# A hybrid SSD and sparse-attention block on one core: the first gate/up pair's products reordered, two operand sums split beside the output projection, the last pair written plainly, the ring moved in four parts, weight memory divided differently

## The chip, the cores and the metric

The kernel runs on one core of a Trainium2 chip. The metric is device time in microseconds (us) of one execution. The engines of the core are named as the profile names them: PE (TensorE matmul), PEld (its weight load), DVE (VectorE), ACT (ScalarE), POOL (GpSimd) and SP (SyncE, which here only issues DMAs). ACT and POOL issue DMAs too.

## The reference

One layer with a batch of 1, 512 tokens, 2048 features, in float32. The first part of the block (projection, SSD mixer, three-branch attention) is the same in both kernels. What matters here is what follows it:

```python
def reference(x, attn_norm_w, w_in, ..., w_out, ffn_norm_w, w_gate, w_up, w_down, final_norm_w):
    h = x
    u = rmsnorm(h, attn_norm_w[l])
    ...
    y_ssd = ssd_mixer(z, xbc, dt_raw, ...)          # 512 x 1024
    y_att = nsa_mixer(q, kc, vc, ks, vs, kw, vw, ...) # 512 x 1024
    mixed = jnp.concatenate([y_ssd, y_att], axis=-1)
    h = h + mixed @ w_out[l]                          # 2048 x 2048
    v = rmsnorm(h, ffn_norm_w[l])
    h = h + (jax.nn.silu(v @ w_gate[l]) * (v @ w_up[l])) @ w_down[l]   # 2048 x 5632, 5632 x 2048
    return rmsnorm(h, final_norm_w)
```

## The kernel before

**Every product is three.** A float32 operand is split into a high part (`a_hi`, ACT, rounds to fp32r) and a low part (`lo`, DVE, the difference to it), and a block of a product is accumulated from high x high, high x low and low x high: lines L1119, L1120 and L1121, one row of 128 x 128 weights at a time.

**The feed-forward part uses seven products for eight.** The matrices are cut into 2 x 2 quarters, and gate, up and down are each computed by seven products `M1` to `M7` of sums of quarters. On the side of the tokens the seven operands are `V0`, `VV` (two) and four sums `T` (index 0 to 3), which POOL forms during the output projection and which are split into high and low parts before the first pair. On the side of the weights the sums are `S1`, `S3`, 11+S1 and 12+11+S1. `S1` and `S3` of gate and up come by a plain DMA and a second, accumulating DMA that POOL issues (L1067). The two others are DVE adds (`plus`, L126).

**Stages.** The input projection, SSD and attention run until about 800 us of the profile, the output projection until about 900. Then come 22 pairs, each of a gate side and an up side of 7 steps (`NP` = 22 tiles of the hidden width). A step is 24 matmuls of 256 columns. The result of a pair, its seven operands for the down projection split in high and low, goes to DRAM as one tile of 1792 KB (`g_d`, `g_forms`). The down projection follows in 36 visits: `VISITS` lists (output block j, number n of hidden tiles), and a visit has seven steps of 3n matmuls.

**The ring.** The down projection reads the tiles of `g_d` back into seven slots (`GRING`), which are the memory of `V0`, `VV` and `T`. `feed(i)` issues the read of tile n on ACT's DMA queue (L1413) two steps after the last step that reads what its slot held (`done`); the slots' order is `V_SLOT`. A read waits for that last step.

**Weights in flight.** Raw weights land in `F` (zone of `NZ` = 56 blocks of 128 x 128, of which the down projection may use the first `NZ2` = 44); the split weights are in `R` (56 blocks). `advance` issues loads on SP (L1065) in the order of `loads`, as soon as a place is free. `form` makes high parts up to three steps ahead, `prep` low parts up to two steps ahead. From the feed-forward part on, each engine's order is that in which the code is written (`manual_schedule`), so an instruction that waits holds up all that stands behind it on its engine.

**First and last pair.** `pair_at_once` runs the first four steps of the first and the last pair as M1, M1, M2, M2 of both sides, then the rest side by side. `start_ff(n)` splits the sums `T`: index 0 and 1 ahead of step 0, index 2 ahead of step 1, index 3 ahead of step 2.

Of the kernel before, what the change touches and what calls it, by code (L numbers as in the profile page):

```python
# [22 lines left out]
VISITS = [(0, 3), (1, 4), (2, 5), (3, 5), (4, 6), (5, 6), (6, 5), (7, 5), (0, 4), (1, 4), (7, 5), (5, 5), (6, 5), (2, 5),  # L23
          (3, 5), (4, 5), (0, 4), (1, 4), (7, 4), (0, 5), (6, 5), (5, 5), (3, 6), (2, 6), (4, 5), (1, 4), (7, 4), (6, 4),
          (0, 6), (1, 6), (7, 4), (2, 6), (6, 3), (5, 6), (4, 6), (3, 6)]
GRING = 7
# [25 lines left out]
NF, NZ, NZ2 = 124, 56, 44  # L52

# [54 lines left out]
def body(ctx, tc, xT, w_in, w_out, w_gate, w_up, w_down, w1k, w1v, cols, rows, kst, out):  # L108
# [46 lines left out]
    g_d = dram.tile([NP, 128, 7, 2, 256], F32, name="g_d")  # L155
# [830 lines left out]
    class Blk:  # L986
# [4 lines left out]
        def __init__(self, n, reads, src=None, plus=None, both=None, inplace=False):  # L991
            self.n, self.reads, self.src, self.plus, self.both, self.inplace = n, reads, src, plus, both, inplace
            self.at, self.down = None, False

        def ap(self):
            return fz.ap(self.at, self.n)

        def read(self):
            self.reads -= 1
            if not self.reads:  # L1000
                fz.free(self.at, self.n)
                self.at = None

    class Zone:


        def __init__(self, key, n):
            self.key, self.busy, self.age, self.now = key, [False] * n, [0] * n, 0
# [4 lines left out]
        def take(self, n, upto, starts=None):  # L1013

            b, g, got = self.busy, self.age, []
            for i in starts or range(upto - n + 1):
                edge = starts or i == 0 or b[i - 1] or i + n == upto or b[i + n] or g[i] != g[i - 1]
                if edge and not any(b[i:i + n]):
                    got.append((max(g[i:i + n]), i))
            if not got:  # L1020
                return None
            a = min(got)[1]
            self.busy[a:a + n] = [True] * n
            return a

        def free(self, i, n):
            self.now += 1
            self.busy[i:i + n] = [False] * n
            self.age[i:i + n] = [self.now] * n


    fz, hz = Zone("F", NZ), Zone("R", NZ)
# [10 lines left out]
    def advance():  # L1043
        while nxt["raw"] < len(loads):
# [3 lines left out]
            if b.inplace:  # L1048
                x, y = b.both
                b.at = x.at  # L1050
# [5 lines left out]
            b.at = place(b)  # L1056
            if b.at is None:
                return
            if b.both:
# [11 lines left out]

    def form(upto):

        while nxt["form"] <= min(upto, len(items) - 1):
            i = nxt["form"]
            b, plus = items[i]
            advance()
            assert b.at is not None, (i, fz.busy)
            if plus is not None:
                add(dve, b.ap(), b.ap(), plus.ap())  # L1080
                plus.read()
            hl[i] = [hl_place(b)]
            assert hl[i][0] is not None, (i, hz.busy)
            a_hi(hz.ap(hl[i][0], b.n), b.ap())
# [652 lines left out]
```

## Time and profile before

| | |
|---|---|
| median of 3 runs | 2320.18 us (2319.45 to 2322.86) |
| the profiled execution | 2321.24 us, its span 2319.3 us |
| busy in the span | PE 2215.3 us, PEld 2057.3, DVE 1803.0, ACT 1098.1, POOL 430.9 |
| DMA | 419.18 MB, 181 GB/s over the span |
| mean granted clock of TensorE | 0.974 |

The profile is of one execution, 2321.24 us long, which is 1.06 us above the median of the runs. About 2 us of it lie outside of the span. Busy shares are means over stages. In the feed-forward part PE's idle time lies in a few stretches, and there the wait that ended last is what counts.

### The profile page before, as it was taken

The page shows a single profiled execution, that of the slowest core. Times are in us where ns is not written, and L with a number is a line of the kernel's source. Part 1 is how long each engine was busy: PE and PEld are TensorE (multiplying, and loading weights), DVE is VectorE, ACT ScalarE, POOL GpSimd, SP SyncE. Part 2 cuts the span into 40 slices and gives each one's busy share as a digit, 9 for nine tenths or more (in the row PEclk, how much of TensorE's full clock was granted, in tenths as well). Part 3 has the DMA queues.
Part 4 walks back from the last instruction along what each step waited for, and adds up shares of the span by engine and source line. Part 5 has one row for each costly group of instructions (what it writes and reads, how often), then busy time and mean ns, then how long its engine had stood idle before and what let it go on. Part 6 is the DMA issues. An engine that isn't in the chain of part 4 may idle for free. (4 is left out here: it accounts for less than half of the span.)

```text
span 2319.3 us, 39808 instructions
## 1 busy us (share of the span) xinstructions
PE 2215.3 (96%) x15376; PEld 2057.3 (89%) x15376; DVE 1803.0 (78%) x2918; ACT 1098.1 (47%) x1767; POOL 430.9 (19%) x439
## 2 busy tenths in 40 slices
PE   7999999999989899999999999999998898999997
PEld 5888888888868678999999999999998898999986
DVE  7699766688797667788888878888785786878776
ACT  4564446566676444444444444444443343333443
POOL 2011334323222233000000010000000121211122
PEclk8999999999999899999999999999999999999998
DMA  4222342222224365878788787878786758676766
GB/s 175 89 69 76 126 137 99 68 89 71 71 83 149 127 220 147 219 216 252 216 250 223 229 235 218 240 210 250 216 251 220 304 168 282 195 258 193 258 162 167
DMA packets 135469, 419.18 MB, mean 181 GB/s; under 512 B 16448, under 2 KB 22096, under 8 KB 129648
## 3 DMA queue, kind: packets, MB, share of 16 engines
q1 hardware_dynamic: 99840, 251.91, 31.3%
q0 software_dynamic: 25776, 77.70, 17.4%
q10 hardware_dynamic: 9664, 87.04, 10.0%
q8 instruction: 120, 1.97, 0.3%
q14 instruction: 69, 0.57, 0.1%
HBM read 354.45 MB, written 58.20 MB: 178 GB/s over the span
## 5 line engine op out<-in xcount | busy, mean ns | idle before, releaser
L117 ACT ACTIVATE R<-F 128x1024 fp32r<-128x1024 f32 (+4 forms) x576 | 517.0, 912 | 668.9 <-DVE F L126 357.7
L120 DVE TENSOR_TENSOR R<-F,R 128x1024 fp32r<-128x1024 f32 (+4 forms) x576 | 610.6, 1067 | 37.8 <-ACT R L117 28.2
L224 PE MATMUL ps_g<-u_hi,whi 128*128 128x512 f32 x592 | 237.5, 401 | 0.0
L226 PE MATMUL ps_g<-u_hi,wlo 128*128 128x512 f32 x592 | 236.1, 399 | 0.0
L225 PE MATMUL ps_g<-u_lo,whi 128*128 128x512 f32 x592 | 235.7, 398 | 0.0
L1121 PE MATMUL ps_s<-T,R 128*128 128x256 f32 x698 | 203.0, 291 | 23.0 <-DVE R L120 23.0
L126 DVE TENSOR_TENSOR F<-F 128x1024 f32<-128x1024 f32 (+4 forms) x168 | 169.9, 1012 | 64.1 <-POOL F L126 39.6
L120 DVE TENSOR_TENSOR wlo<-wraw,whi 128x512 fp32r<-128x512 f32 x196 | 150.6, 771 | 71.2 <-ACT whi L117 70.2
L1121 PE MATMUL ps_g<-T,R 128*128 128x256 f32 x704 | 200.0, 284 | 2.1 <-DVE R L120 2.1
L1119 PE MATMUL ps_s<-T,R 128*128 128x256 f32 x698 | 201.2, 288 | 0.0
L1120 PE MATMUL ps_s<-T,R 128*128 128x256 f32 x698 | 201.1, 288 | 0.0
L1119 PE MATMUL ps_g<-T,R 128*128 128x256 f32 x704 | 199.3, 283 | 1.3 <-ACT R L117 1.1
L1120 PE MATMUL ps_g<-T,R 128*128 128x256 f32 x704 | 199.3, 283 | 0.0
L1121 PE MATMUL ps_t<-T,R 128*128 128x256 f32 x678 | 192.6, 284 | 0.4 <-DVE R L120 0.4
L1120 PE MATMUL ps_t<-T,R 128*128 128x256 f32 x678 | 192.0, 283 | 0.0
L1119 PE MATMUL ps_t<-T,R 128*128 128x256 f32 x678 | 192.0, 283 | 0.0
L117 ACT ACTIVATE whi<-wraw 128x512 fp32r<-128x512 f32 x196 | 122.4, 626 | 141.3 <-PE ps_g L225 92.1
L1121 PEld LDWEIGHTS ps_s<-T,R 128*128 128x128 f32 x698 | 136.7, 196 | 25.3 <-DVE R L120 25.1
L1119 PEld LDWEIGHTS ps_s<-T,R 128*128 128x128 f32 x698 | 136.7, 196 | 0.0
L1120 PEld LDWEIGHTS ps_s<-T,R 128*128 128x128 f32 x698 | 136.6, 196 | 0.0
L1121 PEld LDWEIGHTS ps_g<-T,R 128*128 128x128 f32 x704 | 133.8, 190 | 3.0 <-DVE R L120 2.9
L1119 PEld LDWEIGHTS ps_g<-T,R 128*128 128x128 f32 x704 | 133.6, 190 | 1.7 <-ACT R L117 1.3
(406 smaller groups left out, 6335.9 us busy)
## 6 DMA issues: line engine op xcount, KB each, us to landing
F<-in_w_gate SPq DMA_DIRECT2D x110, 512.0 KB, 5.1
F<-in_w_up SPq DMA_DIRECT2D x110, 512.0 KB, 7.1
wraw<-in_w_in SPq DMA_DIRECT2D x164, 256.0 KB, 3.0
g_d<-F ACTq DMA_DIRECT2D x22, 1792.0 KB, 6.7
F<-in_w_gate POOLq DMA_DIRECT2D x44, 512.0 KB, 6.1
F<-in_w_up POOLq DMA_DIRECT2D x44, 512.0 KB, 5.6
F<-in_w_down SPq DMA_DIRECT2D x68, 320.0 KB, 5.1
T<-g_d ACTq DMA_DIRECT2D x12, 1792.0 KB, 11.8
```

Of the source, the lines that this page charges most:

```text
L117: act.activation(dst, src, AF.Copy, scale=scale)
L120: eng.tensor_tensor(dst, src, f(hi), ALU.subtract)
L126: eng.tensor_tensor(o, a, b, ALU.add)
L224: pe.matmul(p, hi_t[i][:, j, :], ah, start=(k == 0), stop=False)
L225: pe.matmul(p, hi_t[i][:, j, :], al, start=False, stop=False)
L226: pe.matmul(p, lo_t[i][:, j, :], ah, start=False, stop=(k == u.nk - 1))
L1119: pe.matmul(q, h[:, k, :], ah, start=(k == 0), stop=False)
L1120: pe.matmul(q, h[:, k, :], al, start=False, stop=False)
L1121: pe.matmul(q, l[:, k, :], ah, start=False, stop=(k == s.blk.n - 1))
```

## The change

- The first pair's order is now M1, M1, M2, M2, M3, M3, then M6, M7, M5, M4 side by side. Its DVE sums are made for M3 (`sums`), its loads reordered (S1 ahead of 12), and the two steps of the norm (`step_r3`) stand at n = 1 and 4.
- `T` is split in halves (`t_piece`): the first halves of index 0 and 1 beside the output projection (`half_t`, in memory of their own, `ta`), the other six one by one ahead of steps 1 to 6.
- The last pair is written like the pairs in the middle; a slot counts as free after its up side.
- `g_d` is laid out in four slabs, and each DMA moves, per partition, four rows of 3584 bytes in place of one of 14336.
- `R` has 48 blocks in place of 56; 8 blocks `E` serve as further split weights until the down projection, and as further raw weights (`E2`) in it. Split weights in the down projection have eight places of 6 blocks, before it was seven.
- In the first six visits POOL forms S1 in new memory and S3 in place (before the other way round, S3 first). `VISITS` is another list.

```diff
-VISITS = [(0, 3), (1, 4), (2, 5), (3, 5), (4, 6), (5, 6), (6, 5), (7, 5), (0, 4), (1, 4), (7, 5), (5, 5), (6, 5), (2, 5),
...
+VISITS = [(0, 3), (1, 4), (2, 5), (3, 5), (4, 5), (5, 5), (6, 5), (7, 4), (0, 4), (7, 4), (4, 5), (1, 5), (6, 5), (2, 5),
...
+NR, NE = 48, 8
-    g_d = dram.tile([NP, 128, 7, 2, 256], F32, name="g_d")
+    g_d = dram.tile([NP, 4, 128, 896], F32, name="g_d")
...
+    fz, hz, ez = Zone("F", NZ), Zone("R", NR), Zone("E", NE)
     def place(b):
-        return fz.take(b.n, NZ2 if b.down else NZ)
+        n = b.n
+        if b.down:
+            return take(n, fz.find(n, NZ2), ez.find(n) if "E2" in P2 and n <= NE else None)
+        return take(n, fz.find(n))
     def hl_place(b):
-        return hz.take(b.n, NZ, range(0, 42, 6) if b.down else range(0, NZ, 8))
+        n = b.n
+        if b.down:
+            return take(n, hz.find(n, NR, range(0, NR - 5, 6))) or take(n, hz.find(n))
+        return take(n, hz.find(n, NR, range(0, NR, 8)), ez.find(n))
...
+            if c == 7:
+                sch.add(half_t())
+    def t_piece(i, h):
+        src = P2["T1"][h] if i == 0 else (P2["T2"] if i == 1 else P2["T34"][:, i - 2])[:, 4 * h:4 * h + 4]
+        o = P2["T"][i][:, 4 * h:4 * h + 4]
+        a_hi(o[:, :, 0, :], src)
+        lo(dve, o[:, :, 1, :], src, o[:, :, 0, :])
+        if i == 0:
+            fz.free(NZ - 16 + 8 * h, 8)
+    def half_t():
+        yield 12
+        t_piece(0, 0)
+        yield 16
+        t_piece(1, 0)
...
-        nc.scalar.dma_start(g_d[u], f(sg))
+        nc.scalar.dma_start(g_d[u].rearrange("q p n -> p q n"), f(sg).rearrange("p v s t -> p (v s t)").rearrange("p (q n) -> p q n", q=4))
...
+                t_piece(*[(0, 1), (1, 1), (2, 0), (2, 1), (3, 0), (3, 1)][n - 1])
...
+    loads += [qs[0, side][a] for a, side in (("11", 0), ("11", 1), ("S1", 0), ("12", 0), ("12", 1), ("S1", 1), ("S3", 0),
+                                             ("22", 0), ("S3", 1), ("22", 1))]
+    seq = [(0, M1), (1, M1), (0, M2), (1, M2), (0, M3), (1, M3)] + [(i, p) for i in range(2) for p in (M6, M7, M5, M4)]
...
+        if n in (1, 4):
+            ev = step_r3(ev)
...
-    for u in range(1, NP - 1):
+    for u in range(1, NP):
...
-    pair_at_once(NP - 1)
...
-            nc.scalar.dma_start(f(G[n]), g_d[n])
+            nc.scalar.dma_start(f(G[n]).rearrange("p v s t -> p (v s t)").rearrange("p (q n) -> p q n", q=4),
+                                g_d[n].rearrange("q p n -> p q n"))
...
-        add_loads(q, "11 12 21 22 S3 S1" if v < 6 else "11 12 21 22 S1 S3")
+        add_loads(q, "11 12 21 22 S1 S3")
```

Three places show how instructions move. The first is DVE at the start of the first pair, before (T_9071, T_9069, T_9070, T_9072 are index 0 to 3, rows `R<-F,R` the low parts of weights, `F<-F 128x1024` the adds of weight quarters):

```order
L126 TENSOR_TENSOR F<-ps_g,F 128x512
L1181 SCALAR_TENSOR_TENSOR F<-F,colc 128x512
L120 TENSOR_TENSOR T_9071<-F,T_9071 128x4x256 x2
L126 TENSOR_TENSOR acc_97<-ps_v,acc_97 128x512
L120 TENSOR_TENSOR VV<-F,VV 128x2x256
L120 TENSOR_TENSOR T_9069<-F,T_9069 128x8x256
L120 TENSOR_TENSOR R<-F,R 128x1024
L120 TENSOR_TENSOR T_9070<-F,T_9070 128x8x256
L126 TENSOR_TENSOR F<-F 128x1024
L120 TENSOR_TENSOR R<-F,R 128x1024
```

The same place of the changed kernel (T_8420 and T_8421 are index 0 and 1, T_9084 is index 2):

```order
L128 TENSOR_TENSOR F<-ps_g,F 128x512
L122 TENSOR_TENSOR R<-F,R 128x1024
L1204 SCALAR_TENSOR_TENSOR F<-F,colc 128x512
L128 TENSOR_TENSOR acc_97<-ps_v,acc_97 128x512
L122 TENSOR_TENSOR VV<-F,VV 128x2x256
L122 TENSOR_TENSOR T_8420<-F,T_8420 128x4x256
L128 TENSOR_TENSOR F<-F 128x1024 x2
L122 TENSOR_TENSOR R<-F,R 128x1024
L275 TENSOR_SCALAR rst<-ps_m 128x4
L125 TENSOR_TENSOR rst<-rst 128x4 x2
L122 TENSOR_TENSOR T_8421<-F,T_8421 128x4x256
L128 TENSOR_TENSOR F<-F 128x1024 x2
```

A low part of weights has moved up ahead of the sums, the sums come in halves, and the adds of two quarters stand where the adds of one stood.

The second is ACT in the last pair, before (`V`, `VV`, `T` with `<-g_d` are reads of the ring, `R<-F` high parts of weights, L1298 the silu after the gate side):

```order
L1329 DMA g_d<-F 128x3584
L1278 ACTIVATE F<-ps_t 128x256
L117 ACTIVATE R<-F 128x1024
L1413 DMA V_8415<-g_d 128x3584
L117 ACTIVATE R<-F 128x1024 x2
L1413 DMA VV<-g_d 128x3584
L117 ACTIVATE R<-F 128x1024 x4
L1298 ACTIVATE F<-F 128x1024
L117 ACTIVATE R<-F 128x1024 x2
L1413 DMA T_9069<-g_d 128x3584
```

The changed kernel at the same place:

```order
L1371 DMA g_d<-F 128x4x896
L119 ACTIVATE R<-F 128x1024 x5
L1340 ACTIVATE F<-F 128x1024
L119 ACTIVATE R<-F 128x1024
L1320 ACTIVATE F<-ps_g 128x256
L119 ACTIVATE R<-F 128x1024
L1444 DMA V_8415<-g_d 128x4x896
L119 ACTIVATE R<-F 128x1024
L1444 DMA VV<-g_d 128x4x896
L119 ACTIVATE R<-F 128x1024
L1444 DMA T_8421<-g_d 128x4x896
L1452 DMA F<-h_d 128x1024 x2
```

The first two reads of the ring have moved from ahead of the silu to behind it, into the up side, and the first three now follow each other at one step's distance.

The third is SP at the first loads of the down weights, before:

```order
L1065 DMA F<-in_w_up 128x1024 x3
L1065 DMA F<-in_w_down 128x384 x4
L1065 DMA F<-in_w_down 128x512 x4
L1065 DMA F<-in_w_down 128x640 x8
L1065 DMA F<-in_w_down 128x768 x8
L1065 DMA F<-in_w_down 128x640 x10
```

In the changed kernel (E_18322 is `E2`):

```order
L1081 DMA F<-in_w_up 128x1024 x5
L1081 DMA F<-in_w_down 128x384 x4
L1081 DMA F<-in_w_down 128x512 x4
L1081 DMA F<-in_w_down 128x640
L1081 DMA E_18322<-in_w_down 128x640
L1081 DMA F<-in_w_down 128x640 x6
L1081 DMA E_18322<-in_w_down 128x640
L1081 DMA F<-in_w_down 128x640 x12
```

About every sixth load goes to the new place, so one more block of a visit can be under way.

## Rows read from the trace of the kernel before

**Rows 1.** The page: busy tenths of PE in 40 slices of the span.

```profile
PE   7999999999989899999999999999998898999997
```

**Rows 2.** Busy time by stretch: length, engines (instructions), granted clock, DMA share, GB/s.

```profile
900.66:956.87 56.21, 47.14 (x349) 46.32 (x348) 40.81 (x42) 24.30 (x24) 10.47 (x10) 0.88 0.62 160
1050.00:1100.00 50.00, 50.00 (x422) 50.00 (x421) 40.53 (x46) 20.93 (x23) 5.20 (x6) 1.00 0.85 249
1757.27:1810.55 53.28, 42.90 (x339) 42.49 (x338) 32.78 (x38) 16.09 (x20) 3.73 (x4) 0.90 0.72 248
1810.55:1850.00 39.45, 30.66 (x227) 29.63 (x226) 29.95 (x46) 14.56 (x26) 9.76 (x6) 0.91 0.84 338
...
1920.00:1970.00 50.00, 41.47 (x320) 40.66 (x319) 32.05 (x52) 15.53 (x24) 6.81 (x6) 0.90 0.80 289
...
2050.00:2075.00 25.00, 20.90 (x155) 20.70 (x154) 15.78 (x25) 8.52 (x13) 4.94 (x4) 0.86 0.84 291
...
2155.00:2190.00 35.00, 31.60 (x239) 29.86 (x238) 25.04 (x41) 12.29 (x19) 5.88 (x5) 0.95 0.84 288
...
2210.00:2302.40 92.40, 85.09 (x674) 82.14 (x672) 68.22 (x107) 44.22 (x69) 24.97 (x23) 0.98 0.62 144
```

**Rows 3.** DVE in order of time, first pair: start, us, line, what (idle before, releaser).

```profile
889.98 0.69 DVE L126 TENSOR_TENSOR F<-ps_g,F 128x512 f32<-128x512 f32 x1 [1.85 <-PE ps_g L1121]
...
902.32 2.89 DVE L120 TENSOR_TENSOR T<-F,T 128x1024 fp32r<-128x1024 f32 x2
...
905.74 0.68 DVE L120 TENSOR_TENSOR VV<-F,VV 128x512 fp32r<-128x512 f32 x1
907.79 2.29 DVE L120 TENSOR_TENSOR T<-F,T 128x2048 fp32r<-128x2048 f32 x1 [1.38 <-ACT T L117]
...
934.68 1.23 DVE L126 TENSOR_TENSOR F<-F 128x1024 f32<-128x1024 f32 x1 [7.21 <-DMA F<-in_w_up]
```

**Rows 4.** PE in order of time, first pair: its three waits.

```profile
911.28 0.58 PE L1121 MATMUL ps_g<-VV,R 128*128 128x256 f32 x1 [3.63 <-DVE R L120]
...
917.34 0.65 PE L282 MATMUL ps_m<-ident,rst 128*128 128x128 f32 x4 [1.09 <-POOL rst L278]
...
937.10 0.58 PE L1121 MATMUL ps_s<-T,R 128*128 128x256 f32 x1 [4.15 <-DVE R L120]
```

**Rows 5.** POOL in order of time, first and last pair: accumulating loads of S1.

```profile
926.47 0.92 POOL L1067 DMA_DIRECT2D F<-in_w_up  x1 [9.18 <-DMA F<-in_w_up]
...
1780.39 0.86 POOL L1067 DMA_DIRECT2D F<-in_w_up  x1 [25.35 <-DMA F<-in_w_up]
```

**Rows 6.** Packets, MB, share of 16 engines, 1925 to 1945 us; q10 ACT, q1 SP, q0 POOL.

```profile
q10 hardware_dynamic: 544, 7.11, 83.8%
q1 hardware_dynamic: 499, 1.15, 14.6%
q0 software_dynamic: 50, 0.07, 1.9%
```

**Rows 7.** ACT's queue in the last pair: the second read of the ring.

```profile
1770.30 0.33 ACTq L1413 DMA_DIRECT2D VV<-g_d  x1
```

**Rows 8.** DVE at the start of the down projection.

```profile
1810.75 0.69 DVE L126 TENSOR_TENSOR F<-ps_s,F 128x512 f32<-128x512 f32 x1 [3.00 <-PE ps_s L1121]
...
1815.44 0.55 DVE L120 TENSOR_TENSOR R<-F,R 128x384 fp32r<-128x384 f32 x1
```

**Rows 9.** The same view of queues, 810 to 820 us: rows of 2048 and 4096 bytes.

```profile
q1 hardware_dynamic: 1373, 3.96, 100.6%
```

**Rows 10.** The same view, 1970 to 2010 us, where no ring read is under way.

```profile
q1 hardware_dynamic: 2602, 5.85, 48.4%
q0 software_dynamic: 432, 0.98, 14.2%
```

**Rows 11.** POOL: an S1 sum that waits, late in the down projection.

```profile
2223.09 1.82 POOL L126 TENSOR_TENSOR F<-F 128x768 f32<-128x768 f32 x1 [7.83 <-DMA F<-in_w_down]
```

**Rows 12.** What SP's loads waited for, 1810 to 2300 us: us, times, longest.

```profile
SPq L1065 <- DVE R L120: 379.9, 130, 14.3
```

More of the change, by code (lines that the diff above doesn't have):

```diff
@@ L1000, in read, with find @@
             if not self.reads:
-                fz.free(self.at, self.n)
+                self.zone.free(self.at, self.n)
                 self.at = None
     class Zone:
+        now = 0
         def __init__(self, key, n):
-            self.key, self.busy, self.age, self.now = key, [False] * n, [0] * n, 0
+            self.key, self.busy, self.age = key, [False] * n, [0] * n
         def ap(self, at, n):
             return P2[self.key][:, at:at + n, :]
-        def take(self, n, upto, starts=None):
+        def find(self, n, upto=None, starts=None):
             b, g, got = self.busy, self.age, []
+            upto = upto or len(b)
             for i in starts or range(upto - n + 1):
@@ L1075, in form @@
             i = nxt["form"]
-            b, plus = items[i]
+            b, sums = items[i]
             advance()
             assert b.at is not None, (i, fz.busy)
-            if plus is not None:
-                add(dve, b.ap(), b.ap(), plus.ap())
-                plus.read()
+            for x, y in sums:
+                assert all(items[k][0] is not x for k in range(nxt["item"], i))
+                add(dve, x.ap(), x.ap(), y.ap())
+                y.read()
             hl[i] = [hl_place(b)]
             assert hl[i][0] is not None, (i, hz.busy)
-            a_hi(hz.ap(hl[i][0], b.n), b.ap())
+            a_hi(hl_ap(i, 0), b.ap())
             nxt["form"] += 1
@@ L1101, in body, with __init__ @@
     class Step:
-        def __init__(self, blk, rhs, psum, after=None, before=None, plus=None):
+        def __init__(self, blk, rhs, psum, after=None, before=None, sums=()):
             self.i = len(items)
             self.blk, self.rhs, self.psum, self.after, self.before = blk, rhs, psum, after, before
-            items.append((blk, plus))
+            items.append((blk, sums))
             steps.append(self)
@@ L1113, in run_step @@
         n = s.blk.n
-        ats = hl.pop(s.i)
-        h, l = [hz.ap(a, n) for a in ats]
+        h, l = [hl_ap(s.i, a) for a in range(2)]
         p, q = s.psum()
@@ L1122, in run_step @@
             sch.tick()
-        for a in ats:
-            hz.free(a, n)
+        for z, at in hl.pop(s.i):
+            z.free(at, n)
         if s.after:
@@ L1160, in pre_oa @@
         P2["srow"] = P2["SR"].rearrange("p a t -> p (a t)")
+        tp = open_pool("ta", side="right")
+        P2["T"] = {i: tp.tile([128, 8, 2, 256], F32R, name=f"T{i}") for i in range(2)}
+        P2["E"] = open_pool("E", side="right").tile([128, NE, 128], F32R, name="E")
         load_h1(0)
@@ L1393, in body @@
             for n, p in enumerate(SEQ):
-                b, plus = qs[u, side]["form"][p]
-                Step(b, v_rhs(p), bk(p), after=af(p), plus=plus)
-    pair_at_once(NP - 1)
+                b, sums = qs[u, side]["form"][p]
+                s = Step(b, v_rhs(p), bk(p), after=af(p), sums=sums)
+                if (u, side) == (NP - 1, 1):
+                    done[V_SLOT.index(V_OF[p]) - GRING] = s.i
     visits, at_ = [], [0] * NJ
@@ L1557, in d_end, with down_before @@
         return after
-    def down_before(v):
+    def down_before(v, n):
         def before():
-            load_h(v + 1)
+            if n == 1 and v:
+                load_h(v + 1)
+            elif (v, n) == (0, 0):
+                close_pool("E")
+                P2["E2"] = P2["E"] = open_pool("E", side="right").tile([128, NE, 128], F32, name="E2")
         return before
```

98 lines of the change are left out of this document (44 added, 54 removed).

## The prediction, made before the changed kernel ran

> **What bounds the kernel now.** I read the page first: PE's slices are at 9 tenths or more nearly everywhere, and fall lower at the start, around 600 to 700 us, around 800 to 930, and again and again in the last quarter [rows 1]. The change touches nothing before 800 us, so I asked for busy time by stretch behind it. A steady stretch gives the price: 422 matmuls in 50 us, 118.5 ns each, 2.84 us for a step of 24 [rows 2]. Length less count times 118.5 ns is what a stretch loses, slow clock included: first pair 56.2 - 336 x 0.1185 = 16.4 us (13 of its 349 rows are the norm's or its neighbour's); last pair 13.5 us (336 products); the first visits, 1810.6 to 1850, 12.5; 1920 to 1970, 12.1; 2050 to 2075, 6.6; 2155 to 2190, 6.7; 2210 to 2302, 12.5 [rows 2]. That is 80 us, the most that the change can win.
>
> Then the orders of time show what is late in each. **First pair:** PE waits 3.6 us for a low part that stands on DVE behind 2.29 us of splitting T, 1.1 us for the norm, and 4.2 us for the up side's sum 11+S1 [rows 3, 4]. That add waited 7.2 us for its load, whose accumulating half POOL had issued only at 926.5 us [rows 3, 5]. **Last pair:** the same sum is late; POOL waits 25.4 us for the first load of S1 [rows 5], while two ring reads run (the second issued at 1770.3 [rows 7]). How the queues share is seen best around 1935 us: 544 packets of ACT against 499 of SP, but 7.11 against 1.15 MB [rows 6]. Each queue moves a row in turn, and a ring row has 14336 bytes where a weight row of that time has 2560. Weights get 1.15 MB / 20 us = 58 GB/s, and PE runs dry. **Late visits:** no ring read is left; POOL's sum waits for a load [rows 11], and SP's loads wait for DVE to free a place, 380 us in all [rows 12].
>
> **The change, part by part.**
>
> *First pair.* Two halves of T (1.22 us of DVE each at most, half of 2.29 and a start) move beside the output projection, where DVE has gaps of 1.85 us per step [rows 3]: cost nothing; without that cover 1.2 us each. VV was split at 906.4 [rows 3]; with 2.9 us of T gone ahead of it and a low part of some 1.2 us moved there, it is at 904.7. Up to the low part of M3's first step DVE then has half a T, two adds, a low part, half a T, two adds, a low part, eight pieces of about 1.15 us, and some 0.5 us of the norm: 914.4. PE reaches that step at 900.7 + 4 x 2.84 + 0.65 for one group of the norm's products [rows 2, 4] = 912.7. So the wait of 3.6 us shrinks to 1.7. The norm's 1.1 us go, since three steps now lie between its halves. The up side's S1 is the sixth load in place of the eighth, and takes a place that the first split half frees: it lands during the output projection, and the 4.2 us go. Next to be late is S3: its first load follows half a T, at 906; the accumulating load above took 8.2 us (926.5 to 934.7), and with as much for the first it is there at 922, its step at 925: covered. Of the 16.4 us, 8.9 are waits, 1.3 two groups of the norm's products, and 6.2 the slow clock behind the waits; the one wait left keeps 2 of these. Left: 1.7 + 1.3 + 2 = 5. Gain 11; bounds 7 (a second wait like the first) and 14 (no wait).
>
> *Last pair.* With side after side no ring read starts before the up side's first products have ended, 22.8 us in, when its five weight blocks have been issued, as in the pairs between, which lose nothing. The 13.5 us go, but for 0.5: gain 13, bounds 10 and 13.5.
>
> *The ring's rows.* Turn by turn, 3584 against 2560 bytes gives the ring 58%. Rows of 2 and 4 KB reach 396 GB/s [rows 9], against 8.33 MB / 20 us = 417 in the burst [rows 6], so shorter rows cost some 5%. Weights then get 165 GB/s; a visit needs 6 n blocks of 64 KB in 2.49 n us, 158. A tile of 1.835 MB takes 8.0 us, not 4.4 at best. **Starving weights turn into late tiles**, and each burst has to be weighed.
> - *First visits.* A read follows the last product of its slot by about 1 us (the second came at 1770.3, the fourth step ended at 1769.3), so tiles 0 to 2 are issued 23.8, 26.6 and 29.5 us into the pair, and the first product needs tile 2 at 40.5. With about 1.3 MB of weights beside them (places come free one by one), 6.8 MB take 17.2 us: tile 2 lands at 42.5 with 1.5 us of latency. The visit waits anyway for DVE's work on the last pair, 1810.7 to 1816.0 [rows 8], which covers these 2 us. The weights of the fourth visit, late before, come in time. Loss 12.5 to 6.5: gain 6, bounds 2 and 10.
> - *Around 1930 us.* Three tiles again start within two steps; the last is needed some 21 us later. They are 13.9 us of all engines, and weights by themselves take 48.4 + 14.2 = 62.6% [rows 10], 13 us of 21: 27 us of work in 21. Weights can fall behind by what lies in 52 blocks; the rest, 3 to 5 us, is a wait, with 2.5 us of slow clock. Loss 12.1 to 7: gain 5, bounds 0 and 11.
> - *Around 2060 and 2170 us.* The new list needs three tiles in some 20 us each time, and by the same sum loses 5 to 7 us: gain 0, bounds -4 and +10 for both.
>
> *E and the late visits.* A visit has 5 blocks of weights in flight. One place more brings loads forward by a fifth of a visit of 15 us, 3 us, where POOL's sum waited 7.8 [rows 11]: 3/7.8 of 12.5 us is 4.8; some waits are DVE's own, so gain 4, bounds 1 and 9. The order of S1 and S3 on POOL costs nothing, since the third product's sum waits for both either way. The ring's DMAs, four rows per partition, may hold ACT's queue longer than 0.33 us [rows 7]; ACT idles half of the time and works two steps ahead, so 0; at 1 us for each of 44, and none of it covered behind the 15 late tiles, 5 to 15.
>
> Sum: 11 + 13 + 6 + 5 + 0 + 4 = 39 us. From the profiled execution's 2321.2 that is 2282; the median of the runs, 1 us less, gives the same within my rounding.
>
> [...]
>
> **The rivals.**
> - *The split changes no share.* Four rows of 3584 bytes go as one turn. For it: only the counts of long rows are known. Against: short weight rows count one packet each. First and last pair gain their 24 and late visits 4, the bursts lose as before, and the first visits, whose seven reads now all start after the up side's middle, lose 3 more: 2321 - 25 = 2296.
> - *Bursts vanish.* The 52 blocks are slack enough, tiles come in time: 6, 6 and 5 us more at the three bursts and 4 more late, 2282 - 21 = 2261. For it: outside of bursts the DMA engines idle a third of the time [rows 10].
> - *Three queues take turns, and the ring falls to 41%* (3584 of 3584 + 2560 + 2560, POOL's accumulating rows the third). Three tiles take 5.5 MB / (0.41 x 396) = 34 us where 21 are there: 13 us and 2.5 of slow clock at each of three bursts, 46 us in place of the 20 in my sum: 2309. Slower than before it is when the ring gets under some 36%, 39 us for three tiles. For it: POOL takes 14.2% when weights flow [rows 10]. Against: it moves almost nothing in a burst of before [rows 6], and the first visits don't use it.
>
> **How the numbers follow.** Forecast 0.62, its own range 2268 to 2296. Bursts vanish 0.14. No share changes 0.12. Three queues 0.12, of which 0.05 end slower than before and 0.02 near it. 0.2% is about what a measurement of this kernel can tell from no change; its runs lie within 0.15%. The bounds of both pairs and the late visits widen each case by some 6 us; 2261 to 2303 leaves no more than 2 in 10 out. Faster by over 0.2%: 0.93; within 0.2%: 0.02; slower: 0.05.
>
> **What would show it.** First pair about 45 us, no wait for `F<-in_w_up` in it, one short wait at its fifth step. Last pair 40 us. In a burst SP moves as many packets as ACT, at about 40% of the bytes, and PE waits for a read of `g_d` rather than behind POOL sums that wait for `F<-in_w_down`. It is wrong if the ring's share stays near four fifths, if ring DMAs hold ACT's queue so long that high parts come late, or if the last pair still waits for weights.

## The result, and the profile after

The changed kernel takes 2288.14 us (median of 4 runs, 2285.23 to 2292.04), the kernel before in the same comparison 2319.81 (2317.51 to 2322.86): a ratio of 0.9864, 95% interval 0.9844 to 0.9884. Forecast were 2282 and a range of 2261 to 2303. The profiled execution is the slowest of the four: 2292.04 us, span 2290.0, 29.3 us shorter than the span of before.

Stretches of the changed kernel, in the columns of [rows 2]: the middle pairs, first pair, last pair, the first 60 us of the down projection, its three bursts of ring reads, the late visits.

```profile
960.00:1740.00 780.00, 780.00 (x6582) 780.00 (x6581) 643.45 (x724) 349.48 (x392) 67.77 (x79) 1.00 0.81 233
900.56:949.62 49.06, 44.31 (x350) 43.90 (x349) 38.54 (x43) 24.25 (x27) 8.58 (x9) 0.93 0.64 172
1746.21:1785.98 39.77, 39.77 (x338) 39.77 (x337) 31.77 (x37) 15.76 (x19) 5.24 (x5) 1.00 0.84 279
1785.98:1845.98 60.00, 47.81 (x360) 46.18 (x359) 47.86 (x66) 20.78 (x36) 12.94 (x8) 0.91 0.80 299
1900.00:1950.00 50.00, 46.20 (x375) 45.55 (x374) 40.62 (x59) 17.62 (x28) 7.58 (x6) 0.97 0.82 277
2005.00:2030.00 25.00, 19.61 (x154) 19.41 (x154) 16.64 (x28) 8.69 (x13) 2.43 (x2) 0.93 0.98 355
2145.00:2180.00 35.00, 29.43 (x218) 28.61 (x218) 26.12 (x39) 11.01 (x19) 6.81 (x5) 0.91 0.59 182
2180.00:2272.40 92.40, 89.81 (x726) 87.52 (x724) 73.28 (x107) 45.39 (x67) 25.38 (x24) 0.98 0.65 155
```

The first of these stretches in the kernel before:

```profile
960.00:1740.00 780.00, 780.00 (x6551) 780.00 (x6551) 642.79 (x724) 348.74 (x391) 66.64 (x78) 1.00 0.80 232
```

With the prediction's own arithmetic (length less count times 118.5 ns) each of its terms can be set beside what the two profiles show:

| term of the sum | predicted gain (bounds) | measured |
|---|---|---|
| first pair | 11 (7 to 14) | 56.2 to 49.1 us: 7.2 |
| last pair | 13 (10 to 13.5) | 53.3 to 39.8 us: 13.5 |
| first visits | 6 (2 to 10) | loss 12.5 to 17.3: **-4.8** |
| burst near 1930 us (now 1920) | 5 (0 to 11) | loss 12.1 to 5.6: 6.5 |
| two later bursts | 0 (-4 to +10) | loss 13.3 to 15.9: -2.6 |
| E and the late visits | 4 (1 to 9) | loss 12.5 to 6.4: 6.1 |
| the 20 pairs between | not in the sum | 800.4 to 796.6 us: **3.8** |

The measured terms make 29.7 us, the spans 29.3. Two rows are news: the first visits lost where a gain was forecast, and the middle pairs, which the sum held to be untouched, became faster with no wait in them on either side.

PE's longest waits after the change, in order of time, show the rest (columns as in [rows 4]):

```profile
912.26 0.38 PE L1141 MATMUL ps_s<-VV,R 128*128 128x256 f32 x1 [1.90 <-DVE R L122]
918.22 0.58 PE L1141 MATMUL ps_t<-VV,E 128*128 128x256 f32 x1 [2.85 <-DVE E L122]
1790.27 0.38 PE L1139 MATMUL ps_t<-T,R 128*128 128x256 f32 x1 [3.42 <-DMA T<-g_d]
1824.69 0.58 PE L1141 MATMUL ps_g<-V,R 128*128 128x256 f32 x1 [5.51 <-DVE R L122]
1918.06 0.58 PE L1139 MATMUL ps_g<-T,R 128*128 128x256 f32 x1 [2.93 <-DMA T<-g_d]
2023.65 0.58 PE L1139 MATMUL ps_t<-V,R 128*128 128x256 f32 x1 [5.39 <-DMA V<-g_d]
2153.08 0.58 PE L1139 MATMUL ps_g<-V,R 128*128 128x256 f32 x1 [2.90 <-DMA V<-g_d]
```

As forecast, no load of weights is late in the first pair, and in the bursts PE waits for a read of `g_d` instead of a low part. Against the forecast, the first pair has two waits (by the count of products, in its fourth and fifth steps; one was forecast, in the fifth), and the first visits have one for tile 2 and one of 5.5 us.

**What happens in the first visits.** ACT in order of time (rows "ACTq" are DMAs that it issues), then one DVE row:

```profile
1774.79 0.42 ACTq L1444 DMA_DIRECT2D T<-g_d  x1
...
1790.31 0.38 ACTq L1444 DMA_DIRECT2D T<-g_d  x1
1790.73 0.53 ACT L119 ACTIVATE R<-F 128x384 fp32r<-128x384 f32 x1 [11.12 <-DVE F L1362]
...
1792.26 3.62 ACTq L1444 DMA_DIRECT2D T<-g_d  x1
...
1804.85 0.61 ACTq L1452 DMA_DIRECT2D F<-h_d  x1
```

```profile
1822.81 0.42 DVE L128 TENSOR_TENSOR F<-ps_s,F 128x256 f32<-128x256 f32 x1 [5.77 <-DMA F<-h_d]
```

The third read of the ring (tile 2) is issued at 1774.79 and takes 15.4 us, so it lands at 1790.19, and PE's wait ends at 1790.27. The fifth read, whose step on PE had ended at 1780.3, is issued at 1790.31, within 0.1 us of that landing; ACT had stood still for 11.1 us. (The view names a DVE instruction that ended at 1790.26. In the program the activation waits for an earlier one, an add that ended at 1782.4; what held it is the read ahead of it in ACT's order.) Three reads then start within 2 us, and the load of `h_d` behind them in ACT's queue takes 17.9 us. DVE waits 5.8 us for it, and so PE 5.5.

Why would the fifth read wait for the third? The program says so. These are the DMAs of the place in ACT's order, with the semaphores that they wait for:

```
1357 L1444 DMA T1_8421<-g_d_68 128x4x896
1358 L1452 DMA F_8354<-h_d_67 128x1024 [waits DMAHW1_49,DVE_49]
1359 L1452 DMA F_8354<-h_d_67 128x1024 [waits DMAHW3_49]
1361 L1444 DMA T2_9084<-g_d_68 128x4x896 [waits DMAHW4_49,PE_49]
1363 L1444 DMA T0_8420<-g_d_68 128x4x896 [waits DMAHW6_49,PE_49]
```

In the program every DMA that SP or ACT issues counts up one of eight semaphores, `DMAHW0` to `DMAHW7`, in turn, and waits until the DMA that used it eight before has landed. The third read counts up `DMAHW6`, and the fifth is the eighth DMA behind it. SP's weight loads are caught in the same way. What they waited for from 1760 to 1830 us (us, times, longest); no data tie a weight load into F to a read into VV or T:

```profile
SPq L1081 <- DVE R L122: 45.6, 12, 9.3
...
SPq L1081 <- DMA VV<-g_d: 6.9, 2, 6.5
SPq L1081 <- DMA T<-g_d: 5.0, 1, 5.0
```

### The profile page after: what moved, and what is told of

It is laid out like the page before. It is cut to its first block, busy times and chain, and to the rows that moved or that the text cites. A ratio compares the mean times of both kernels' runs of the same rounds, so it can differ in the third digit from the quotient of the medians.

```text
span 2290.0 us, 39809 instructions
## 1 busy us (share of the span) xinstructions
PE 2202.2 (96%) x15376; PEld 2044.9 (89%) x15376; DVE 1813.9 (79%) x2921; ACT 1092.2 (48%) x1770; POOL 428.0 (19%) x439
## 5 line engine op out<-in xcount | busy, mean ns | idle before, releaser
L119 ACT ACTIVATE R<-F 128x1024 fp32r<-128x1024 f32 (+4 forms) x538 | 485.2, 922 | 605.0 <-DVE F L128 341.1
L122 DVE TENSOR_TENSOR R<-F,R 128x1024 fp32r<-128x1024 f32 (+4 forms) x430 | 454.3, 1063 | 32.4 <-ACT R L119 28.2
L1139 PE MATMUL ps_g<-T,R 128*128 128x256 f32 x696 | 197.2, 283 | 2.9 <-DMA T<-g_d 2.9
L1140 PE MATMUL ps_g<-T,R 128*128 128x256 f32 x696 | 197.2, 283 | 0.0
L1139 PE MATMUL ps_t<-T,R 128*128 128x256 f32 x689 | 193.5, 281 | 3.4 <-DMA T<-g_d 3.4
L1139 PE MATMUL ps_s<-T,R 128*128 128x256 f32 x695 | 196.6, 283 | 0.0
L1140 PE MATMUL ps_s<-T,R 128*128 128x256 f32 x695 | 196.1, 282 | 0.0
L1140 PE MATMUL ps_t<-T,R 128*128 128x256 f32 x689 | 193.4, 281 | 0.0
L128 DVE TENSOR_TENSOR F<-F 128x1024 f32<-128x1024 f32 (+5 forms) x146 | 153.9, 1054 | 16.1 <-POOL F L128 12.1
L1141 PE MATMUL ps_g<-T,R 128*128 128x256 f32 x576 | 163.6, 284 | 0.3 <-DVE R L122 0.2
L1141 PE MATMUL ps_t<-T,R 128*128 128x256 f32 x577 | 162.7, 282 | 1.1 <-DVE R L122 1.0
L122 DVE TENSOR_TENSOR E<-F,R 128x1024 fp32r<-128x1024 f32 x108 | 132.3, 1225 | 4.7 <-ACT R L119 4.5
L228 PEld LDWEIGHTS ps_g<-u_hi,wlo 128*128 128x128 f32 x592 | 111.5, 188 | 24.4
L1139 PEld LDWEIGHTS ps_t<-T,R 128*128 128x128 f32 x689 | 129.9, 189 | 3.6 <-DMA T<-g_d 3.6
L1140 PEld LDWEIGHTS ps_s<-T,R 128*128 128x128 f32 x695 | 132.6, 191 | 0.0
```

The source lines that it names most:

```text
L119: act.activation(dst, src, AF.Copy, scale=scale)
L122: eng.tensor_tensor(dst, src, f(hi), ALU.subtract)
L128: eng.tensor_tensor(o, a, b, ALU.add)
L228: pe.matmul(p, lo_t[i][:, j, :], ah, start=False, stop=(k == u.nk - 1))
L1139: pe.matmul(q, h[:, k, :], ah, start=(k == 0), stop=False)
L1140: pe.matmul(q, h[:, k, :], al, start=False, stop=False)
```

## The experiments

All compute the whole layer. Ratios are to the kernel before.

| run | median us (range, runs) | ratio, 95% interval |
|---|---|---|
| e1, long rows | 2288.94 (2286.2 to 2290.95, 4) | 0.9867, 0.9851 to 0.9882 |
| e2, h_d by POOL | 2280.97 (2280.58 to 2282.14, 4) | 0.9834, 0.9820 to 0.9847 |
| e3, ring by POOL | 2300.24 (2294.94 to 2301.82, 5) | 0.9913, 0.9897 to 0.9930 |
| e4, old list | 2290.28 (2288.32 to 2292.09, 4) | 0.9873, 0.9859 to 0.9887 |
| e5, T shifted (on before) | 2311.48 (2308.1 to 2320.9, 8) | 0.9967, 0.9949 to 0.9985 |
| e6, plain last pair (on before) | 2343.08 (2333.53 to 2345.51, 7) | 1.0098, 1.0081 to 1.0115 |
| e7, old division | 2304.38 (2300.81 to 2306.73, 6) | 0.9928, 0.9912 to 0.9944 |
| e8, e2 and shifts | 2282.74 (2278.55 to 2287.47, 5) | 0.9838, 0.9819 to 0.9857 |
| e9, no E2 | 2308.23 (2306.61 to 2311.35, 5) | 0.9952, 0.9938 to 0.9966 |
| e10, pieces later | 2282.36 (2278.19 to 2283.43, 4) | 0.9837, 0.9823 to 0.9850 |
| e11, first seven long | 2286.54 (2285.33 to 2288.74, 4) | 0.9859, 0.9846 to 0.9873 |
| e12, T at 64 (on before) | 2311.62 (one run) | |

**e1: ring rows long again.**

```diff
-    g_d = dram.tile([NP, 4, 128, 896], F32, name="g_d")
+    g_d = dram.tile([NP, 128, 7, 2, 256], F32, name="g_d")
...
+            nc.scalar.dma_start(f(G[n]), g_d[n])
```

> The changed kernel with g_d in one slab again: a ring row has 14336 bytes in place of 3584, nothing else differs. By the prediction's rows theory the ring's share of bytes in a burst goes back from 63 to 80 % or more, weight loads land in 12 us in place of 7.5, PE's waits in the bursts turn from waits for a read of g_d into waits behind weights, and the burst near 1908 us loses 5 us more; tile 2 lands some 3 us earlier at the first visits. Time 2285 to 2295, middle 2290. Rival, rows change no share: the profile of the bursts and the time stay as they are, 2288. On the late reads of the first visits: if a DMA must wait for the one that used its completion counter eight DMAs before, the fifth read is still issued within 0.1 us of the landing of the third (which was so at 1790.3 us); if it waited for room in ACT's queue, which holds a quarter of the rows now, it is issued when its own step has ended, near 1783 us.

Measured: the same time within the intervals, but not the same stages. The first 60 us of the down projection lose 13.2 us (395 products) in place of 17.3, and the first burst has one wait of 6.4 us for a low part where the changed kernel waits 2.9 us for a tile. In the 140 us behind the first 60, PE loses 10.2 us where it lost 6.3. So the split wins 4 us in the burst and gives 4 back at the first visits. What the queues moved in 15 us from the start of this burst's three reads, first the changed kernel, then e1:

```profile
q10 hardware_dynamic: 1255, 4.38, 78.4%
q1 hardware_dynamic: 470, 1.08, 18.4%
```

```profile
q10 hardware_dynamic: 363, 4.75, 79.9%
q1 hardware_dynamic: 260, 0.62, 10.5%
```

Over these 15 us the ring's share of the two is 80% with short rows and 88% with long ones, and weight loads land in 8.2 us in place of 13.9. But the 15 us are not all alike. The changed kernel from 1902 to 1908 us and from 1908 to 1911, then e1 from 1896 to 1911:

```profile
q10 hardware_dynamic: 432, 1.49, 63.0%
q1 hardware_dynamic: 411, 0.94, 40.2%
```

```profile
q10 hardware_dynamic: 350, 1.20, 101.5%
q1 hardware_dynamic: 10, 0.01, 1.2%
```

```profile
q10 hardware_dynamic: 419, 5.32, 83.6%
q1 hardware_dynamic: 415, 0.96, 16.3%
```

While both queues have rows to move, they move as many of each, with short rows as with long ones: the ring then has 61% of the bytes with short rows (1.49 of 2.43 MB) and 85% with long ones. The 80% comes from stretches in which SP's queue is empty. SP issued three loads up to 1899.69, whose rows moved from 1901.5 to 1908.3, and then stood still until 1907.37 because no place was free (the view names DVE); the rows of the next loads moved from 1910.9 on.

The fifth read again waited for the third, with a quarter of the rows in the queue (PE's row for tile 2 and the read itself, in e1):

```profile
1785.54 0.39 PE L1139 MATMUL ps_t<-T,R 128*128 128x256 f32 x1 [0.96 <-DMA T<-g_d]
```

```profile
1785.57 0.33 ACTq L1444 DMA_DIRECT2D T<-g_d  x1
```

That is the counter, not a lack of room.

**e2: h_d's loads by POOL.**

```diff
-        nc.scalar.dma_start(P2["H"][j][:, 1:5, :], h_d[j])
+        nc.gpsimd.dma_start(P2["H"][j][:, 1:5, :], h_d[j])
```

> The changed kernel with the loads of h_d (512 KB each) issued by POOL in place of ACT. Counter theory: two DMAs fewer lie between the third and the fifth read of the ring, so that the fifth no longer shares the third's counter: it is issued at 1783 to 1786 us in place of 1790.3, ACT's wait of 11.1 us goes, and DVE's wait of 5.8 us for h_d, which stood in ACT's queue behind four reads, goes too. First visits lose 9 to 12 us in place of 17.6: time 2278 to 2283. Rival, no room in ACT's queue: the fifth read stays at 1790, only the wait for h_d goes, 5 us: 2283 to 2285. Rival, bytes alone bind the first visits: the same bytes have to land, PE waits as long, 2288.

Measured 2281, all its runs below all of the changed kernel's. Two reads of the ring and the wait for tile 2, in e2:

```profile
1775.99 4.62 ACTq L1444 DMA_DIRECT2D T<-g_d  x1
...
1790.30 0.37 ACTq L1444 DMA_DIRECT2D VV<-g_d  x1
```

```profile
1790.27 0.58 PE L1139 MATMUL ps_t<-T,R 128*128 128x256 f32 x1 [5.93 <-DMA T<-g_d]
1805.08 0.38 PE L1141 MATMUL ps_t<-V,R 128*128 128x256 f32 x1 [0.87 <-DVE R L122]
```

With the two loads gone from ACT, the fifth read is no longer eighth behind the third and goes 10 us earlier against the first visit, which starts at 1781.82 here; now the sixth (VV) is, and it is issued 0.03 us behind PE's row for tile 2. That moves the wait just as the counters say. The wait for `h_d` is gone; the first visits lose 12.8 us (398 products in 60 us). But tile 2 still lands at 1790 and took 19.6 us in place of 15.4: the reads that are no longer held up go beside it, and from the first read's issue to that landing all queues moved 9.0 MB in place of 7.4.

**e3: the ring by POOL.** `nc.gpsimd.dma_start` in place of `nc.scalar.dma_start` for the reads of `g_d`.

> The changed kernel with all reads of the ring issued by POOL in place of ACT. They then use POOL's completion counters, so neither SP's weight loads nor ACT wait for them: waits of SP's loads for reads of g_d (5 to 9 us at each burst) are gone. Counter theory: the seven first reads are issued as their steps end, from 1769 to 1788 us, first visits lose 10 us in place of 17.6, the bursts 2 us less each: 2276. Rival, POOL is held: a read of 512 rows takes POOL some us to issue where 128 rows took 0.9, and its sums stand behind it; at 3 us for each of 15 reads, half of it uncovered, 2288 + 20 = 2308. Rival, bytes bind: 2288.

Measured 2300, and not by the price that the rival gave: a read holds POOL for 0.75 to 1.15 us. SP waited for no ring read any more from 1786 us on, as the counters say. But the first visits lose 17.9 us (355 products in 60 us) where 10 were expected, and reads now stand behind POOL's sums. POOL near the second burst, and PE's wait for that read:

```profile
2018.97 1.57 POOL L128 TENSOR_TENSOR F<-F 128x640 f32<-128x640 f32 x1 [16.14 <-DMA F<-in_w_down]
2020.48 0.77 POOL L1444 DMA_DIRECT2D V<-g_d  x1
```

```profile
2028.47 0.58 PE L1139 MATMUL ps_t<-V,R 128*128 128x256 f32 x1 [7.94 <-DMA V<-g_d]
```

The sum waits 16 us for weights, the read behind it comes 8 us too late. PE waits 27.8 us for ring reads in all (changed kernel 14.6).

**e4: the old list of visits.** `VISITS` of the kernel before.

> The changed kernel with the visits of the kernel before. The prediction's sum gave the list no gain of its own (bursts near 2060 and 2170 us lose the same): 2288, bounds 2282 to 2294, with the burst of three reads 27 us after the first product of the down projection in place of 22. Rival, the list is what won at the first burst and in the late visits: these lose 12 us as in the kernel before, 2295 to 2300. First visits have the same first four entries: unchanged, 17.6 us.

Measured 2290.3, 2 us above the changed kernel and within the runs' spread; the down projection's products take 484.9 us in place of 485.6. The list by itself is worth nothing that can be measured, as the sum had it.

**e5 and e12: T shifted in the kernel before.**

```diff
+                tp.tile([128, 8], F32, name="pad")
                 P2["T"] = {i: tp.tile([128, 8, 2, 256], F32R, name=f"T{i}") for i in (1, 2, 0, 3)}
```

> The kernel before with 32 unused bytes ahead of the four tiles T, nothing else. In the program the split weights R begin at byte 85824 of each partition, 64 above a multiple of 128, as the four T do; V0 and VV lie 96 above one. In the trace of before the 24 products of a step take 119.7 to 120.0 ns each where the operand is a T, and 118.0 to 118.3 where it is V0 or VV. Theory of offsets: a product is slower by 1.5 ns when weights and operand stand at the same offset. Shifted to 96, the T steps take 118.2, the middle pairs 39.7 us in place of 40.0, the pairs end 6 us earlier and the down projection gains 2 to 3: 2310 to 2313. Rival, the gain of 0.2 us per pair in the changed kernel comes from its other weight places or from the pairs' order: 2319, rates as before.

For e12 the pad is twice as long.

> The kernel before with 64 unused bytes ahead of the four tiles T, so that they begin 0 above a multiple of 128 (before 64, like R; with 32 bytes 96). Theory that only the same offset as the weights' is slow: T steps at 117 ns, as with 32 bytes. Rival, a period of 64 bytes: T steps at 120 ns, as before. Second rival, it is the distance of T from V0 and VV that counts, since these slowed from 118 to 120 ns when T was shifted: neither.

Measured: e5 2311.5, e12 2311.6 in its one run. The middle stretch of e5, then of e12:

```profile
960.00:1740.00 780.00, 780.00 (x6608) 780.00 (x6607) 647.25 (x728) 351.48 (x393) 66.52 (x77) 1.00 0.81 233
```

```profile
960.00:1740.00 780.00, 780.00 (x6634) 780.00 (x6634) 648.94 (x730) 351.36 (x394) 67.36 (x78) 1.00 0.81 234
```

6551, 6608 and 6634 products in the same 780 us at full granted clock: 119.1, 118.0 and 117.6 ns each. No instruction differs but in an address. By operand (means over the pairs, from the starts of PE's rows): before, T 119.8 to 120.0 and V0/VV 117.9 to 118.2 (single steps of these 117.2 to 118.8); e5, T 116.7 and V0/VV 119.9 to 120.0; e12, all 117.2 to 117.8. The 20 middle pairs take 800.4 us before, 793.6 in e5 and 790.4 in e12. That the address counts is shown by these rates; by the times alone it would be weaker, since three of e5's eight runs (2318 to 2321) lie at the level of the kernel before. The theory that the offset of operand and weights decides is not: in e5 V0 and VV slowed down without having moved.

**e6: the plain last pair alone, on the kernel before.**

```diff
-    for u in range(1, NP - 1):
+    for u in range(1, NP):
...
-    pair_at_once(NP - 1)
```

> The kernel before with only the last pair written like the pairs between. The prediction's term: the last pair takes 40 us in place of 53.3, gain 13. The ring's reads start later against the first visits, which lose 13 us as with long rows in the changed kernel (before: 12.8): 2304 to 2308. Rival, the work only moves: reads and weights of the first visits come later by as much as the pair is shorter, first visits lose 20 us or more, 2312 to 2319.

Measured 2343, **slower than before by 1%** (the profiled execution, at the fast end of its runs, spans 2331.8 us). The last pair does take 40.0 us, with the rate of the kernel before. The down projection takes 29.6 us more (538.4 in place of 508.7): the first visits lose 17.1 us in place of 12.6, which is between the expectation and its rival, and about half of the loss, 15.5 us, is 430 us later. The late visits of e6, to be set beside the last of [rows 2], and one of their two waits of about 6 us on PE with what ACT waited for:

```profile
2220.00:2312.40 92.40, 73.75 (x543) 70.82 (x544) 56.44 (x89) 36.35 (x56) 19.74 (x20) 0.91 0.54 127
```

```profile
2233.95 0.58 PE L1119 MATMUL ps_t<-T,R 128*128 128x256 f32 x1 [5.79 <-ACT R L117]
```

```profile
2233.05 2.72 ACT L117 ACTIVATE R<-F 128x768 fp32r<-128x768 f32 x4 [8.85 <-DMA F<-in_w_down]
```

543 products in place of 674 in the same length: a loss of 28 us in place of 12.5. The order of loads is fixed, and each takes the first place in F that is free. A last pair written otherwise leaves other places free, and by the programs this goes on through all visits. Counted in the programs: how many steps before its first use the latest load of a visit gets its place (visits 29 to 36):

```
before             4 4 5 4 5 5 4 4
e6 plain last      4 4 5 1 4 1 3 3
e7, e9             4 5 5 4 5 1 3 3
changed kernel     6 7 5 5 5 5 4 4
```

In e6 and e9 each 1 stands in a visit with such a wait (5.8 and 6.3 us in e6, 5.9 in e9).

**e7 and e9: the weight memory.** e7 takes `NR, NE = 56, 0`, seven places for split weights in the down projection and 44 blocks for raw ones; e9 only takes E from the raw weights:

```diff
-        return take(n, fz.find(n, NZ2), ez.find(n) if "E2" in P2 and n <= NE else None)
+        return take(n, fz.find(n, NZ2), None)
```

> The changed kernel with the weight memory of the kernel before: R has 56 blocks, no E, seven places of 6 blocks for split weights in the down projection, 44 blocks for raw ones. The prediction's term for E: the late visits lose 4 us more (bounds 1 and 9): from 320 us after the first visit's start on they lose 20 in place of 16; time 2290 to 2294. By the theory of offsets T2 and T3 stay slow with R, T0, T1, V0 and VV fast: 118.6 ns in the pairs, as in the changed kernel. Rival, a place more for raw weights is worth nothing, since DVE and the ring decide: 2288.

> The changed kernel with E closed in the down projection: raw weights keep the 44 blocks of F, all else as changed (split weights have their eight places). Theory of places: the loads get the very places and steps that they had with the old division (the load behind a sum of the 34th visit gets its place one step ahead of its use, where the changed kernel has five), so the loss of the old division comes from these 8 blocks: 2300 to 2305. Rival, it came from the split weights' places (eight against seven): 2288 to 2292.

Measured 2304.4 and 2308.2. Without the 8 blocks the changed kernel loses 20 us, five times my term; the places for split weights gain nothing that can be seen. Where e9 and e7 have a load one step ahead of its use, e9 has this wait:

```profile
2245.56 0.58 PE L1139 MATMUL ps_s<-T,R 128*128 128x256 f32 x1 [5.85 <-ACT R L119]
```

This wait and the slow clock behind it (0.94 granted from 2200 to 2292 us, 0.98 in the changed kernel's late visits) are a part of the loss only: in the profiles e9's down projection takes 23.3 us more than the changed kernel's, 10.7 of them in the late visits. That the rest also comes from places is argued, not shown.

In e7's pairs, where all split weights lie in one block of memory, the steps with T2 and T3 took 119.2 to 119.8 ns and all others 117.2 to 117.5, so e7's middle pairs are 4 us faster than the changed kernel's; this was not expected, and it is as much as e7 is faster than e9 by.

**e8: e2 with two shifts of 32 bytes.** A pad ahead of T2 and T3 and one ahead of E.

> The changed kernel with h_d's loads on POOL and two shifts of 32 bytes: T2 and T3 from offset 64 to 96, E from 96 to 64, so that every operand lies at 96 and every split weight at 64. Theory of offsets: all steps at 118.0 to 118.2 ns, pairs 3 us shorter in sum, down projection 1 to 2 us: 2276 in place of 2281. Rival, offsets don't matter: 2281, rates of steps unchanged.

Measured 2282.7, no gain on e2. The rate went from 118.5 to 118.4 ns only, where the theory of offsets had 118.0 to 118.2 for all steps: it fails here a second time.

**e10: the pieces of T later.**

```diff
-        Step(..., before=start_ff(n) if n < 7 else None, sums=sums)
+        Step(..., before=start_ff(n) if n < 9 else None, sums=sums)
...
-                t_piece(*[(0, 1), (1, 1), (2, 0), (2, 1), (3, 0), (3, 1)][n - 1])
+                at = {1: (0, 1), 4: (1, 1), 5: (2, 0), 6: (2, 1), 7: (3, 0), 8: (3, 1)}
+                if n in at:
+                    t_piece(*at[n])
```

> The changed kernel with the pieces of T ahead of other steps: the second half of index 0 stays ahead of step 1, the five others stand ahead of steps 4 to 8 in place of 2 to 6. The second wait of the first pair, 2.85 us for the low part of the up side's M3, stood on DVE behind a piece of 1.23 us and its wait of 0.74 us for ACT: it falls to 0.9 us, and the slow clock behind it by 1 us. First pair 45 to 46 us, the second half of T2 and T3 still in time. Time 2285 to 2286. Rival, the adds alone decide (2.48 us of DVE ahead of the low part): the wait stays 2.8, 2288.

Measured 2282.4. The low part that PE waits for, on DVE, and PE's wait:

```profile
911.15 2.48 DVE L128 TENSOR_TENSOR F<-F 128x1024 f32<-128x1024 f32 x2
913.55 1.22 DVE L122 TENSOR_TENSOR E<-F,R 128x1024 fp32r<-128x1024 f32 x1
```

```profile
914.82 0.39 PE L1141 MATMUL ps_t<-VV,E 128*128 128x256 f32 x1 [0.92 <-DVE E L122]
```

The wait is 0.9 us as forecast. (It is in the fifth step, the gate side's M3, and not in the up side's as the expectation says.) The first pair takes 44.1 us at a granted clock of 1.00 (changed kernel: 49.1 at 0.93; in e1 to e4, where the first pair is the same code, 45.8 to 47.1 at 0.96 to 1.00, so the profiled run of the changed kernel had a slow one). That is 2 to 3 us of the 5.8 us between the medians; where the rest comes from is open. In the profiles the down projection, whose code is the same, is 2.2 us shorter, which is within what single profiles differ by.

**e11: long rows for the first seven tiles, on e2.** Tiles below `GRING` are written and read in rows of 14336 bytes, the others as changed.

> The changed kernel with h_d's loads on POOL and the first seven tiles of g_d in rows of 14336 bytes, the other fifteen in rows of 3584. The first visits want their three tiles before weights, the bursts weights before tiles. With long rows tile 2 landed 2 us behind the first visit's start in place of 8.5: the wait of 5.9 us falls to 2 at most, first visits lose 9 in place of 13; the bursts lose as with short rows, 6.8 in the first: 2276 to 2278. Rival, bytes alone bind the first visits: long rows give tile 2 early and weights late, 13 again, 2281.

Measured 2286.5, 6 us slower than e2: a miss. Tile 2 still came 3.8 us late, and the five loads of weights beside the reads landed in 16.6 to 25.6 us where e2's took 8.5, so later waits of 2.8 and 3.2 us for low parts took the place of what was won. First visits lose 16.5 us where e2 lost 12.8, the expectation had 9 and the rival 13. The rival had the kind of thing right, tile 2 earlier and weights late, but not the size: who goes first moved the wait and made it longer.

## Why the prediction was right, and where it was not

- **The sign and size** (forecast 2282, measured 2288) came from the pairs: 20.7 us of the 29.3, for which 24 were forecast. No waits, full clock and 39.8 us in the last pair are as the text had them. That the total came near is in part luck: of the 39 us three terms were 17.2 us too high (first pair, first visits, later bursts), and what came in more than forecast elsewhere, 7.9 us, made up for nearly half.
- **First pair, 11 against 7.2.** The sum followed DVE up to the low part of M3's first step, the pair's fifth, and had it ready at 914.4 and PE there at 912.7: one wait of 1.7 us. The two low parts that PE waits for, on DVE:

```profile
910.99 1.22 DVE L122 TENSOR_TENSOR R<-F,R 128x1024 fp32r<-128x1024 f32 x1
916.95 1.22 DVE L122 TENSOR_TENSOR E<-F,R 128x1024 fp32r<-128x1024 f32 x1
```

  The first is that of the fourth step, the up side's M2. It stands in the same chain, behind half a T and two adds, and the sum did not ask when PE needs it: 1.9 us. The second is M3's: it ended at 918.17, 3.8 us later than summed (VV was split at 906.2 in place of 904.7, and DVE stood 1.6 us in the chain for ACT's high parts of T), and PE waits 2.85 us. Behind this wait the granted clock was 0.56 (918.2 to 925 us), behind the first 1.00 (912.3 to 917). My lower bound named a second wait. e10 takes the second half T out of this chain, brings the 2.85 us to 0.9 and reaches the 44 to 45 us of the forecast.
- **First visits, 6 against -4.8: the step that failed.** It took the reads to be issued as their steps end, and let 6.8 MB take 17.2 us to tile 2. Tile 2 came at 44.0 us of the pair against 42.5 forecast, a small miss. The 1.5 us of latency in that forecast came with no row; in the trace of before, with ACT's queue empty ahead of them, the first row of a ring read moved 1.6 us behind its issue at 1800.26 and 2.2 us behind that at 1922.52. What the step lacked is, first, that a DMA waits for another through a shared counter: reads five to seven were held to 1790, came in a lump, and delayed `h_d`. e2 undoes this and wins back 4.5 of the 10.8 us by which the term was off. The other 6.3 us stay in e2, where PE waits 5.9 us for tile 2. "The visit waits anyway for DVE's work" did not hold: PE waited for the read, 3.4 us in the changed kernel. That this wait is the bytes' own is likely, not shown: from the first read's issue to the landing of tile 2 all queues moved 7.4 MB (9.0 in e2, where more reads go beside it), at about 400 GB/s from 1773 us on; e2, e3 and e11 move the wait and don't remove it, and no run had fewer bytes there.
- **Bursts, 5 against 6.5, and 0 against -2.6.** Weights did land earlier (8.2 us in place of e1's 13.9) and tiles became late (PE waits 2.9, 5.4 and 2.9 us for them), as said. The rule of turns held: while both queues had rows, they moved 432 and 411 of them, the ring had 61% of the bytes (58% forecast) and weights 157 GB/s (165 forecast). What the sum did not see is that SP's queue was empty for a part of the first burst (10 rows from 1908 to 1911 us), because its loads waited for places; so the ring's share of that burst's 15 us did stay at 80%, near the four fifths that the prediction had named as a sign of being wrong. Its rival "the split changes no share" gets no support from that, since with both queues at work the share fell from 85% to 61%. e1's equal time is that rival's result by another way: the split wins 4 us at the first burst and loses 4 at the first visits. That rival's own ground, four short ring rows to one weight row, is not in the trace (432 to 411). How many rows of each queue make a turn no run counted.
- **E and the late visits, 4 against 6.1: right by accident.** The sum let each part count for itself. e6 and e9 show that it does not: the plain last pair alone spoils the places of the late loads (28 us lost there in e6's profile, 12.5 before) and makes the kernel slower, and the changed kernel without E's blocks is 20 us slower (e9). So the 13.5 us of the last pair are a gain of its stage, not what that part of the change is worth by itself, and E is worth five times my 4 beside it. E without the plain last pair was not run.
- **What was not in it:** 3.8 us of the middle pairs, where the step price of 118.5 ns from one stretch of 50 us hid that the kernel before ran at 119.1 ns over 780. e5 and e12 show that T's addresses are enough for it.

Fastest of these versions is e2, 2281 us; e10 is next with 2282. The two together, and either with e12's address, were not run.

## What to carry to other kernels

A term for a stage is good only while the memory planner's state, which the stage hands on, stays what it was: time each part alone and both together, and count how many steps ahead of its use each load gets its place. Read the share of two queues only where both have something to move: a mean over a burst also counts the time in which one of them is empty (80% here, 61% with both at work). Look up which DMAs share a completion counter before you start long transfers among short ones: here, eight DMAs later, ACT stood still for 11.1 us, and SP waited 6.5 us for a ring read with which its load shares no data. And take the price of a steady step from the longest stretch that is steady (here 118.5 ns over 50 us, 119.1 over 780).

## What the runs showed of the hardware that was not expected

A product of 128 x 128 weights with 256 columns at full granted clock took from 116.7 to 120.0 ns by step, and only addresses in the on-chip memory differed: moving four operand tiles by 32 or 64 bytes made the 20 middle pairs of the kernel before 6.8 and 10.0 us shorter (its time: a ratio of 0.9967, interval 0.9949 to 0.9985, and one run at 2311.6 us). With T at 64 bytes more all seven kinds of steps took 117.2 to 117.8 ns. These runs show a dependence of up to 2.8% on where the operands lie. Which pair of addresses decides is open: equal offsets in 128 bytes fit the kernel before, e7, e12 and most steps of the changed one, not e5's V0 and VV nor e8.

A DMA queue with rows of 3584 bytes and one with rows of 2560 moved 432 and 411 rows in 6 us while both had work, and with rows of 14336 bytes 419 and 415 in 15 us (e1): rows, not bytes, were shared evenly.

The times of one stretch also differ between profiles of the same code: the first pair took 45.8 to 49.1 us, with the granted clock at 1.00 in the shortest and 0.93 in the longest.
